# Another work order, a fourth load buffer and three conditioning pieces on TensorE in a hybrid decoder layer

## The chip, the cores and the metric

One core of one Trainium2 chip runs the whole layer. The metric is device time in microseconds (us), the lower the better. Five engines run their own instruction queues in order and wait for each other by semaphores: PE (TensorE, matmuls), DVE (VectorE), ACT (ScalarE), POOL (GpSimd) and SP (SyncE), which here issues nearly all DMA transfers.

## The reference

A decoder layer for 256 tokens of width 1024, in float32. A vector c gives six vectors (shift, scale and gate for two sublayers). The first sublayer is a token mixer with four gated DeltaNet heads and four HGRN2 heads, the second a mixture of 64 experts, 8 per token, with one shared expert. Cut to what matters:

```python
mod = c_act @ w_ada + b_ada                     # c_act = silu(c); w_ada is 1024 x 6144
sh1, sc1, g1, sh2, sc2, g2 = split(mod, 6)
h = rms_norm(x, norm1_w) * (1 + sc1) + sh1
x = x + g1 * token_mixer(h)                     # below
h = rms_norm(x, norm2_w) * (1 + sc2) + sh2
x = x + g2 * moe(h)                             # sigmoid router, top 8 of 64, plus a shared expert
return rms_norm(x, final_norm_w)

def token_mixer(h):
    proj = h @ w_in                             # 1024 -> q, k, v, gate A, beta, a, f, i, q B, gate B
    q, k, v = causal_short_conv(proj[:1536])    # 4 taps, silu
    oA = gated_delta_chunked(l2(q), l2(k), v, g, beta)       # chunks of 64, triangular solve
    oA = rms_norm(oA) * silu(gateA)
    oB = hgrn2_chunked(silu(qB), kB, iB, logf)               # kB, logf from sigmoid(f)
    oB = rms_norm(oB) * silu(gateB)
    return concat(oA, oB) @ w_out
```

## The kernel before

The kernel has two stages, the mixers and the experts.

**Mixers.** All work up to the residual behind the out-projection is cut into small pieces. Each piece is a step of a Python generator (up to its next `yield`), and the string `SEQ` names the generators in the order in which their steps are written: `W4` splits a block of w_in's rows, `Q4` multiplies it, `c1` is a step of a conditioning piece, `s_f0` a split of a weight tile, `inv` a step of the triangular inverse, `g0` and `g1` steps of the HGRN2 recurrence. Since each engine runs its queue in order, `SEQ` sets what stands before what on every engine. The table `ENG` says for some element-wise steps whether DVE or POOL does them, and `BANKS` which pair of PSUM banks a step uses.

Weights come in halves of 1 MB (128 partitions x 2048 floats), two halves to a tile `ld`, of which there are three buffers. They are queued on SP in the order in which `SEQ` first names them, and `take` issues them up to `NLD` = 6 halves ahead of the one that is needed. A tile takes the buffer of the tile three before it, so a load may stand on SP until that buffer has been read.

To keep float32 precision at the speed of the rounded type, a weight is split: ACT casts the high part (L451, L428) and DVE or POOL subtracts it for the low part (L452, L429). Three matmuls (high x high, high x low, low x high) then make each product: `first_columns` (L438, tiles `pqk`) for the first 1024 columns of w_in, 8 row blocks of 24 matmuls each, and `piece` (L477) for v, f, qb, i, gA and gB.

The conditioning has two halves. sh1 and sc1 are needed before the first projection: `ada` (L395) multiplies the blocks A0 to A3 of w_ada by c, 16 matmuls with 32 output columns each (32 passes on the array in the timeline's count), copies the sums (L398) and turns them to columns (L402); block Aq gives the columns of row blocks 2q and 2q + 1 of h. The other four vectors are made by eight pieces c0 to c7 (`cond`, tiles `ldc`): ACT scales the first slab, then seven steps on DVE add the others,

```python
S.activation(pa, t[:, :, 0, :], AF.Copy, scale=cact[:, 0:1])                      # L874
for j in range(1, 8):
    engine(f"c{n}", "V").scalar_tensor_tensor(pa, t[:, :, j, :], cact[:, j:j + 1], pa, ...)  # L877
TE.matmul(pc, lhsT=ones, rhs=pa, start=True, stop=True)                           # L880
V.tensor_tensor(dst, dst, two(pc), op=ALU.add)                                    # L882
```

`ba` (L496) makes beta and the decay, `ml` (L599) and `dec` (L616) the decay matrices, `LB` (L646) masked blocks for the inverse, `hT` (L413) the low part of h, `sgt` (L905) the gates' product, `out_part` (L1035) the out-projection, `xa` (L1063) a product of the second norm, whose result is `hpt` (L1070).

**Experts.** Behind the second norm the routing is computed (transposes L1159, logits L1227), while PE does the shared expert's gate and up (L1185); its weights take the tile `wbl0`, which reuses a load buffer (L1141, L1142). The weights of two experts are loaded ahead of the routing (`gu` and `wbl`, L995). Then 49 planned places are filled with the experts that are used, in the order of their load: gate, up and down matrices of 1 MB each stream through six pairs of buffers (`wbl`, `wbp`, `gu`) and five for the down matrices (`wbs`, `wbd`, `dn`), issued by L1370 to L1385, and the helper at L1399 does the matmuls. The last norm ends the kernel.

Of the kernel before, what the change touches and what calls it, by code (L numbers as in the profile page):

```python
# [40 lines left out]
NLD = 6  # L41
# [29 lines left out]
)  # L71

ENG = {
# [86 lines left out]
def tile_layer(ctx, tc, x, small, rows, w_ada, w_in, w_out, b_ada, gdn_norm_w, hg_norm_w, norm2_w, w_router, router_bias,  # L160
# [36 lines left out]
    x_sb = keep.tile([P, 2, D], F32, name="x_sb")  # L197


    loads, tiles, issued = [], {}, [0]  # L200

    def queue(key, half, src):
        loads.append((key, half, src))

    def issue(upto):
        while issued[0] < min(upto, len(loads)):
            key, half, src = loads[issued[0]]
            if half is None:
# [1497 lines left out]
```

## Time and profile before

| | us |
|---|---|
| median of 3 runs (lowest, highest) | 651.94 (649.45, 652.8) |
| the profiled execution, whole | 653.51 |
| its span in the trace | 651.6 |
| busy: PE, weight loads, DVE, ACT, POOL | 591.7, 367.4, 300.3, 209.8, 122.8 |

The shares of the whole span hide that the stages differ: DVE has 46% of the span, but most of that lies in the first third. The rows further below are therefore read stage by stage: the front (until the first projection is done, 61.6 us), the middle (the rest of the mixers, until the last out-projection matmul at 233.0), the tail (until the routing is known and the first planned expert load is issued, 256.4), and the experts. A row of a timeline that has x32 stands for 32 instructions, its first start and the time from there to the last end.

### The profile page before, as it was taken

The numbers are of one execution on the slowest core, as the hardware profiler recorded it, in microseconds if no ns is written. First come the engines' busy times: TensorE is split into PE (matmuls) and PEld (weight loads), VectorE is DVE, ScalarE is ACT, GpSimd is POOL, SyncE is SP. The second block draws the span as 40 slices with busy tenths as digits, with TensorE's granted clock in tenths as the row PEclk, the third lists the DMA queues.
The fourth block names the chain that finished last, engine by engine and source line by source line (L and its number), as shares of the span: only waits on it lengthen the run. The fifth ranks groups of instructions, "written<-read, shape, count | busy, mean of one in ns | idle before, by whom it ended". The sixth has DMA issues, their size and how long they took to land.

```text
span 651.6 us, 13055 instructions
## 1 busy us (share of the span) xinstructions
PE 591.7 (91%) x5317; PEld 367.4 (56%) x5318; DVE 300.3 (46%) x608; ACT 209.8 (32%) x409; POOL 122.8 (19%) x150
## 2 busy tenths in 40 slices
PE   3799887778898969999999999999999999999982
PEld 1499877777797957644445555444444444555321
DVE  4368999969899866112122221212221212221144
ACT  3356786535375451111112122121211111112112
POOL 7025255536474632000000000000000000000001
PEclk9889998969999989999999999999999999999997
DMA  8986563626638393999999999999999999999961
GB/s 344 422 336 245 194 259 130 208 82 233 257 132 351 135 351 137 421 391 412 420 420 419 420 420 420 420 418 417 420 420 418 421 419 420 419 418 420 418 228 69
DMA packets 32739, 216.78 MB, mean 333 GB/s; under 512 B 3792, under 2 KB 4128, under 8 KB 7456
## 3 DMA queue, kind: packets, MB, share of 16 engines
q1 hardware_dynamic: 32576, 215.83, 81.7%
q8 instruction: 44, 0.72, 0.5%
q14 instruction: 23, 0.19, 0.1%
q10 hardware_dynamic: 96, 0.04, 0.0%
HBM read 214.81 MB, written 1.05 MB: 331 GB/s over the span
## 4 chain that ended last, share of the span: by engine, by line
PE 62%; DVE 18%; DMA 13%; issue 3%; ACT 2%; SPq 1%; DVEq 0%; ACTq 0%
PE pgum L1399 21%; PE pym L1399 11%; PE pgm L1399 6%; PE acc L1399 6%; DVE pacc L877 4%; PE pqk L438 3%; DMA ldA<-in_w_ada_dram 3%; DMA wbl<-in_w_up_dram 3%; DMA wbp<-in_w_up_dram 3%; DMA wbd<-in_w_down_dram 3%; DVE cacc L542 2%; DVE wps L452 2%; PE i L477 2%; PE pgs L1185 2%; PE gA L477 2%
## 5 line engine op out<-in xcount | busy, mean ns | idle before, releaser
L1399 PE MATMUL pgum<-wbl,xgm 128*32 128x512 f32 (+1 forms) x768 | 155.3, 593 | 0.0
L1399 PE MATMUL pgum<-wbp,xgm 128*32 128x512 f32 (+1 forms) x448 | 98.7, 593 | 1.1 <-DMA wbp<-in_w_up_dram 1.1
L1399 PE MATMUL pym<-wbs,hTtm 128*32 128x512 f32 (+1 forms) x288 | 83.5, 596 | 0.5 <-ACT hTtm L1508 0.5
L1399 PEld LDWEIGHTS pgum<-wbl,xgm 128*32 128x32 f32 (+1 forms) x768 | 43.0, 113 | 67.3 <-issue 66.5
L1167 DVE TENSOR_TENSOR hhm<-sgm,pgum 128x256 f32<-128x256 f32 x24 | 14.9, 619 | 140.7 <-ACT sgm L1165 140.7
L1569 POOL TENSOR_TENSOR o<-x_sb,fbc 128x512 f32<-128x512 f32 x2 | 2.5, 1272 | 385.2 <-DVE x_sb L1551 385.2
L1535 DVE SCALAR_TENSOR_TENSOR ylm<-pym,gcm,yhm 128x512 fp32r<-128x512 f32 x46 | 34.6, 751 | 69.1 <-ACT yhm L1534 69.1
L1399 PE MATMUL pgum<-gu,xgm 128*32 128x512 f32 (+1 forms) x160 | 63.5, 593 | 0.0
L1399 PE MATMUL pym<-wbd,hTtm 128*32 128x512 f32 (+1 forms) x296 | 61.7, 595 | 0.5 <-ACT hTtm L1508 0.5
L1165 ACT ACTIVATE sgm<-pgum 128x256 f32<-128x256 f32 x24 | 9.2, 385 | 154.8 <-PE pgum L1399 154.8
L877 DVE SCALAR_TENSOR_TENSOR pacc<-ldc,cact,pacc 128x512 f32<-128x512 f32 x56 | 56.5, 1009 | 1.0
L1534 ACT ACTIVATE yhm<-pym,gcm 128x512 fp32r<-128x512 f32 x46 | 31.6, 688 | 76.1 <-PE pym L1399 76.1
L1399 PEld LDWEIGHTS pgum<-wbp,xgm 128*32 128x32 f32 (+1 forms) x448 | 26.4, 113 | 39.6 <-issue 39.6
L1399 PE MATMUL pym<-dn,hTtm 128*32 128x512 f32 (+1 forms) x104 | 43.5, 596 | 0.0
L1399 PE MATMUL pgm<-smm,h2hi 128*128 128x256 f32 x192 | 43.3, 305 | 0.0
L1399 PE MATMUL pgm<-smm,h2lo 128*128 128x256 f32 x192 | 38.2, 280 | 0.0
L1399 PE MATMUL acc<-yhm,stm 128*128 128x512 f32 x98 | 34.0, 427 | 0.0
L1399 PEld LDWEIGHTS pym<-wbs,hTtm 128*32 128x32 f32 (+1 forms) x288 | 20.2, 113 | 21.5 <-issue 19.5
L1399 PE MATMUL acc<-ylm,stm 128*128 128x512 f32 x94 | 29.9, 396 | 0.2 <-DVE ylm L1532 0.2
L1399 PEld LDWEIGHTS pgm<-smm,h2lo 128*128 128x128 f32 x192 | 29.5, 188 | 0.2 <-issue 0.2
L1399 PEld LDWEIGHTS pgm<-smm,h2hi 128*128 128x128 f32 x192 | 29.4, 189 | 0.3 <-issue 0.2
L1399 PEld LDWEIGHTS acc<-yhm,stm 128*128 128x128 f32 x98 | 16.5, 188 | 22.8 <-issue 18.8
(458 smaller groups left out, 1073.0 us busy)
## 6 DMA issues: line engine op xcount, KB each, us to landing
wbl<-in_w_gate_dram SPq DMA_DIRECT2D x25, 1024.0 KB, 17.4
wbl<-in_w_up_dram SPq DMA_DIRECT2D x25, 1024.0 KB, 19.4
wbs<-in_w_down_dram SPq DMA_DIRECT2D x19, 1024.0 KB, 15.4
wbd<-in_w_down_dram SPq DMA_DIRECT2D x19, 1024.0 KB, 19.2
wbp<-in_w_gate_dram SPq DMA_DIRECT2D x17, 1024.0 KB, 17.5
wbp<-in_w_up_dram SPq DMA_DIRECT2D x17, 1024.0 KB, 19.5
ldc<-in_w_ada_dram SPq DMA_DIRECT2D x16, 1024.0 KB, 7.9
dn<-in_w_down_dram SPq DMA_DIRECT2D x10, 1024.0 KB, 16.5
```

What stands on the lines that cost most here:

```text
L438: TE.matmul(pqk[m // 2][:, (m % 2) * T:(m % 2) * T + T], lhsT=ws[j][PAIRS[k][0]][:, m * P:m * P + P], rhs=hT[:, PAIRS[k][1], j, :], start= ...
L452: engine(f"s_{key}{q}", "GGVG"[q]).tensor_tensor(lo, t[:, 2 * q:2 * q + 2, :], hi.bitcast(F32), op=ALU.subtract)
L477: TE.matmul(pj[:, i * T:i * T + T], lhsT=lh, rhs=rh, start=(i == 0 and j == 0 and k == 0), stop=(i == 1 and j == 7 and k == 2), skip_group ...
L542: V.scalar_tensor_tensor(acc, xp[:, k:k + T], convcol[:, 12 * k + blk:12 * k + blk + 1], acc, op0=ALU.mult, op1=ALU.add)
L877: engine(f"c{n}", "V").scalar_tensor_tensor(pa, t[:, :, j, :], cact[:, j:j + 1], pa, op0=ALU.mult, op1=ALU.add)
L1165: S.activation(sg, pgate[:, 0:FE], AF.Silu)
L1167: V.tensor_tensor(hh.rearrange("p j q -> p q j"), sg.rearrange("p (q j) -> p q j", j=2), pgate[:, FE:2 * FE].rearrange("p (q j) -> p q j", ...
L1185: TE.matmul(pg2[:, i * FE:i * FE + FE], lhsT=hT_all[j // 4][:, j % 4, b * P:b * P + P], rhs=gu[:, i, j * FE:j * FE + FE], start=(j == 0 an ...
L1399: last_pe[0] = fn(*args, **kw).ins
L1534: S.activation(yh, pyd, AF.Copy, scale=gc)
L1535: V.scalar_tensor_tensor(yl, pyd, gc, yh.bitcast(F32), op0=ALU.mult, op1=ALU.subtract)
L1569: G.tensor_tensor(o[b, n], x1[:, b, sl], fbc[:, sl], op=ALU.mult)
```

## The change

The string `SEQ`, the tables `ENG` and `BANKS` are replaced as wholes, and with them the order of all the mixers' work. Of the split subtractions 11 instead of 19 are on DVE and 53 instead of 45 on POOL. On POOL instead of DVE are also one `xa` product, one `dec` product, two `LB` products and one `hT` subtraction; on DVE instead of POOL two of the `ml` products and one `sgt` product. `FIRST` orders the row blocks of the first projection: 6, 7, 4, 5, 0, 1, 2, 3. There are four buffers of load tiles, and `NLD` is 8; a load is written only where the last step that reads its buffer's previous tile stands ahead of it in `SEQ` (`lastread`). The conditioning pieces c0, c1 and c6 (`COND_PE`) are made by 16 matmuls, a copy by ACT, two matmuls that gather the sums, and the same addition as before. In the experts' stage one pair of buffers comes from the load pool instead of its own; there are six as before.

```diff
--- before.py
+++ after.py
-NLD = 6
+NLD, NLDBUF = 8, 4
...
-    "ba z0 par par par x A3 x xT0 xT0 A3 A3 xT1 xT1 A2 A2 A2 xT3 xT3 h7 xT2 h7 xT2 h5 h5 A0 A0 A0 h1 h1 h4 h4 z0 "
...
+    "par par x x xT0 xT3 xT1 xT3 A3 xT2 A3 A3 xT2 A2 h6 h6 h7 A2 W6 h7 A2 h4 xT1 Q6 W7 Q6 Q6 z0 A1 Q7 A1 xT0 Q7 A1 h5 Q7 W4 "
...
+COND_PE = (0, 1, 6)
+
+FIRST = (6, 7, 4, 5, 0, 1, 2, 3)
...
-    ld = ctx.enter_context(tc.tile_pool(name="load", bufs=3))
+    ld = ctx.enter_context(tc.tile_pool(name="load", bufs=NLDBUF))
...
-    loads, tiles, issued = [], {}, [0]
+    loads, tiles, issued, wanted = [], {}, [0], [0]
+    slots, lastread = [], {}
 
     def queue(key, half, src):
         loads.append((key, half, src))
 
-    def issue(upto):
+    def issue(upto, at=None):
+
         while issued[0] < min(upto, len(loads)):
             key, half, src = loads[issued[0]]
             if half is None:
                 row_loads(key)
             else:
                 if key not in tiles:
+                    if at is not None and len(slots) >= NLDBUF and lastread[slots[-NLDBUF]] > at:
+                        return
+                    slots.append(key)
                     tiles[key] = ld.tile([P, 2, 8, 256], F32, name=f"ld{key}", tag="ld")
                 SY.dma_start(out=tiles[key][:, half, :, :].rearrange("p j n -> p (j n)"), in_=src)
             issued[0] += 1
 
     def take(key, half, shape=None):
         n = next(n for n, l in enumerate(loads) if l[:2] == (key, half))
-        issue(n + NLD)
+        issue(n + 1)
+        wanted[0] = max(wanted[0], n + NLD)
         return half is not None and tiles[key][:, half, :, :]
+
+
+    count = {}
+    for place, op in enumerate(SEQ.split()):
+        seen = count.get(op, 0)
+        count[op] = seen + 1
+        if op[0] == "A" and op[1:].isdigit() and seen == 0:
+            lastread[op] = place
+        elif op[0] == "W" and seen == 0:
+            lastread[f"W{int(op[1:]) // 4}"] = place
+        elif op[:2] == "s_" and seen == 3:
+            lastread[op[2:-1]] = place
+        elif op[0] == "c" and op[1:].isdigit() and seen == (0 if int(op[1:]) in COND_PE else 7):
+            lastread[op] = place
+        elif op[0] == "y" and op[1] in "AB" and seen == 1:
+            lastread[f"wo{int(op[2]) // 2}"] = place
...
-    issue(NLD)
+    issue(NLD, 0)
+    wanted[0] = NLD
...
-    crep = tmp.tile([P, 8, 32], F32, name="crep", tag="a0")
+    crep = cp.tile([P, 8, 32], F32, name="crep")
...
-        if j in (3, 7):
-            hi, lo = (ep.tile([P, 1024], F32R, name=f"spw{j}{n}", tag=tag) for n, tag in enumerate(("attT", "LT")))
+        place = FIRST.index(j)
+        if place in (3, 7):
+            hi, lo = (ep.tile([P, 1024], F32R, name=f"spw{place}{n}", tag=tag) for n, tag in enumerate(("attT", "LT")))
         else:
-            if j == 2:
+            if place == 2:
                 w = mp.tile([P, 2, 1024], F32R, name="spw2", tag="kv8")
             else:
-                w = sps[(0, 1, 0, 0, 0, 1, 0)[j]].rearrange("p (a n) -> p a n", a=2)
+                w = sps[(0, 1, 0, 0, 0, 1, 0)[place]].rearrange("p (a n) -> p a n", a=2)
...
-                          start=(m % 2 == 0 and j == 0 and k == 0), stop=(m % 2 == 1 and j == 7 and k == 2), skip_group_check=True)
+                          start=(m % 2 == 0 and j == FIRST[0] and k == 0), stop=(m % 2 == 1 and j == FIRST[-1] and k == 2), skip_group_check=True)
...
+        if n in COND_PE:
+            pm = bank(f"cm{n}", "pm")
+            for j in range(4):
+                for g in range(4):
+                    k = 4 * (g % 2) + j
+                    TE.matmul(pm[32 * g:32 * g + 32, 0:256], lhsT=crep[:, k, :], rhs=t[:, g // 2, k, :], start=(j == 0), stop=(j == 3))
+            yield
+            pmc = tmp.tile([P, 256], F32, name=f"pmw{n}", tag="cacc")
+            (V.tensor_copy if ENG.get(f"cm{n}") == "V" else S.copy)(pmc, pm[:, 0:256])
+            yield
+            pc = bank(f"c{n}", "pm")
+            for i in range(2):
+                TE.matmul(pc[:, 256 * i:256 * i + 256], lhsT=pick[:, i:i + 1].to_broadcast([P, P]), rhs=pmc, start=True, stop=True)
+            yield
+            V.tensor_tensor(dst, dst, two(pc), op=ALU.add)
+            return
...
-                              start=(nm == "B" and n % 2 == 0 and j == 0 and k == 0), stop=(nm == "A" and n % 2 == 1 and j == 3 and k == 2),
-                              skip_group_check=True)
+                              start=(npy[n // 2, b] == 0), stop=(npy[n // 2, b] == 47), skip_group_check=True)
+                    npy[n // 2, b] += 1
...
-    for op in SEQ.split():
+    for place, op in enumerate(SEQ.split()):
         if op not in started:
             started[op] = WORK[op]()
         next(started[op], None)
+        issue(wanted[0], place)
...
-    lds = [ld.tile([P, 2, 2048], F32, name=f"wbl{k}", tag="ld") for k in range(3)]
-    wps2 = [wp2.tile([P, 2, 2048], F32, name=f"wbp{k}", tag="wp", bufs=2) for k in range(2)]
-    pairs = [lds[0], ahead[0][0], lds[1], wps2[0], wps2[1], lds[2]]
+    lds = [ld.tile([P, 2, 2048], F32, name=f"wbl{k}", tag="ld") for k in range(4)]
+    pairs = [lds[0], ahead[0][0], lds[1], lds[2], wp2.tile([P, 2, 2048], F32, name="wbp"), lds[3]]
...
-    sr = tmp.tile([P, 2, NE], F32, name="sr", tag="sr", bufs=1)
+    sr = tmp.tile([P, 2, NE], F32, name="sr", tag="m8", bufs=1)
```

SP's queue at the start of the program, weight loads of w_ada (A, c) and w_in (W, f); x2 means both halves, 1 MB each. Before:

```order
L213 DMA ldA3_100<-in_w_ada_dram 128x2048 x2
L213 DMA ldA2_103<-in_w_ada_dram 128x2048 x2
L213 DMA ldA0_106<-in_w_ada_dram 128x2048 x2
L213 DMA ldA1_228<-in_w_ada_dram 128x2048 x2
L213 DMA ldW0_271<-in_w_in_dram 128x2048 x2
L213 DMA ldc0_318<-in_w_ada_dram 128x2048 x2
L213 DMA ldW1_354<-in_w_in_dram 128x2048 x2
```

After:

```order
L220 DMA ldA3_100<-in_w_ada_dram 128x2048 x2
L220 DMA ldA2_103<-in_w_ada_dram 128x2048 x2
L220 DMA ldW1_106<-in_w_in_dram 128x2048
L220 DMA ldA1_108<-in_w_ada_dram 128x2048 x2
L220 DMA ldW1_106<-in_w_in_dram 128x2048
L220 DMA ldA0_253<-in_w_ada_dram 128x2048 x2
L220 DMA ldW0_286<-in_w_in_dram 128x2048 x2
L220 DMA ldc0_432<-in_w_ada_dram 128x2048 x2
```

W1, whose half with row blocks 6 and 7 now comes before A1, stood behind all four A tiles, W0 and c0; A0 now comes after A1 and all of W1.

POOL's queue where the f, qb and v projections begin (`wps` is the low part of a split weight, `ldf`, `ldqb`, `ldv` its source, T5, L5 and X32 tiles of the inverse). Before:

```order
L452 TENSOR_TENSOR wps0_81<-ldf_460,wps0_81 128x512
L452 TENSOR_TENSOR wps1_82<-ldqb_463,wps1_82 128x512
L632 MEMSET T5_207 128x1024
L632 MEMSET L5_208 128x512
L452 TENSOR_TENSOR wps0_81<-ldf_460,wps0_81 128x512
L452 TENSOR_TENSOR wps1_82<-ldf_460,wps1_82 128x512 x2
L452 TENSOR_TENSOR wps0_81<-ldqb_463,wps0_81 128x512
L452 TENSOR_TENSOR wps1_82<-ldqb_463,wps1_82 128x512 x2
L616 TENSOR_TENSOR dec_726<-dec_726,lex_123 128x4x128
L452 TENSOR_TENSOR wps0_81<-ldv_900,wps0_81 128x512
L646 TENSOR_TENSOR LB_205<-LT_203,bd32_146 128x128 x2
```

After:

```order
L478 TENSOR_TENSOR wps0_81<-ldf_436,wps0_81 128x512
L658 MEMSET T5_345 128x1024
L478 TENSOR_TENSOR wps0_81<-ldf_436,wps0_81 128x512
L478 TENSOR_TENSOR wps1_82<-ldqb_501,wps1_82 128x512 x2
L478 TENSOR_TENSOR wps0_81<-ldf_436,wps0_81 128x512 x2
L478 TENSOR_TENSOR wps1_82<-ldqb_501,wps1_82 128x512 x2
L642 TENSOR_TENSOR dec_728<-dec_728,lex_126 128x4x128
L478 TENSOR_TENSOR wps0_81<-ldf_436,wps0_81 128x512
L658 MEMSET L5_346 128x512
L478 TENSOR_TENSOR wps0_81<-ldf_436,wps0_81 128x512
L691 COPY X321_937<-ident32_148 128x256
L478 TENSOR_TENSOR wps0_81<-ldqb_501,wps0_81 128x512
```

Ahead of the first `LB` product, which waits for DVE, there were eight splits of f and qb; now there are thirteen, and with them a split of v, two `dec` products and the copy X32 among them.

PE's queue at the end of the mixers (`py` are the out-projection's sums, `ph` the second norm's transposes, `pgs` the shared expert's gate). Before:

```order
L1035 MATMUL py00_2548<-wps1_82,oTA_2727 128x256 x12
L1035 MATMUL py10_2583<-spoA20_2561,oTA_2727 128x256 x6
L1035 MATMUL py10_2583<-spoA21_2628,oTA_2727 128x256 x6
L1035 MATMUL py10_2583<-spoA30_2642,oTA_2727 128x256 x6
L1035 MATMUL py10_2583<-spoA31_2697,oTA_2727 128x256 x6
L1159 MATMUL ph00_2945<-ident_109,hpt_2873 128x128 x4
L1159 MATMUL ph01_2951<-ident_109,hpt_2873 128x128 x4
L1159 MATMUL ph10_2957<-ident_109,hpt_2873 128x128 x4
L1159 MATMUL ph11_2963<-ident_109,hpt_2873 128x128 x4
L1185 MATMUL pgs0_2941<-wbl0_2909,hpt_2873 128x256
```

After:

```order
L1078 MATMUL py00_2563<-wps1_82,oTA_2700 128x256 x12
L1078 MATMUL py10_2657<-spoA30_2713,oTA_2700 128x256 x6
L1078 MATMUL py10_2657<-spoA20_2583,oTA_2700 128x256 x6
L1078 MATMUL py10_2657<-spoA31_2763,oTA_2700 128x256 x6
L1078 MATMUL py10_2657<-spoA21_2697,oTA_2700 128x256 x6
L904 MATMUL cm6_2885<-ldc6_2248,crep_163 32x256 x16
L911 MATMUL c6_2904<-pmw6_2902,pick_173 128x256 x2
L1202 MATMUL ph00_2978<-ident_112,hpt_2863 128x128 x4
L1202 MATMUL ph01_2984<-ident_112,hpt_2863 128x128 x4
L1202 MATMUL ph10_2990<-ident_112,hpt_2863 128x128 x4
L1228 MATMUL pgs0_2974<-wbl0_2942,hpt_2863 128x256
L1202 MATMUL ph11_2996<-ident_112,hpt_2863 128x128 x4
```

The matmuls of c6 now stand between the last out-projection matmul and the transposes, and the first `pgs` matmul, which reads `wbl0`, ahead of the last transposes.

## Rows read from the trace of the kernel before

**Rows 1.** Windows by stage: busy us (x instructions) of each engine, granted clock, DMA share, GB/s.

```profile
32.80:61.60 28.80, 28.80 (x222) 27.55 (x223) 21.47 (x34) 15.87 (x23) 9.46 (x8) 0.93 0.71 274
...
233.00:256.40 23.40, 17.08 (x98) 13.22 (x98) 14.88 (x63) 9.23 (x16) 7.68 (x5) 0.93 0.61 248
256.40:624.20 367.80, 366.08 (x2743) 176.66 (x2742) 84.26 (x180) 69.89 (x133) 0.00 (x0) 1.00 1.01 416
624.20:651.60 27.40, 14.54 (x102) 5.08 (x102) 10.51 (x22) 6.89 (x15) 2.50 (x2) 0.87 0.28 103
```

**Rows 2.** Chain of waits, its end: start us, us, what.

```profile
604.14 19.93 DMA wbp<-in_w_up_dram
...
624.20 7.04 PE pgum L1399 x58
```

**Rows 3.** Timeline of PE, front: start, us, line, out<-in, count [idle before <-releaser].

```profile
17.10 1.93 PE L395 MATMUL A<-ldA,crep 128*32 128x256 f32 x32
...
27.78 3.62 PE L395 MATMUL A<-ldA,crep 128*32 128x256 f32 x28 [2.56 <-DMA ldA<-in_w_ada_dram]
...
32.81 7.72 PE L438 MATMUL pqk<-hT,wps 128*128 128x256 f32 x48
...
42.28 2.90 PE L496 MATMUL ba<-hT,wbs 128*8 128x256 f32 x24
```

**Rows 4.** Windows, the front's loads.

```profile
0.00:16.00 16.00, 5.89 (x37) 2.67 (x39) 6.71 (x22) 5.82 (x10) 12.47 (x55) 1.00 0.87 344
16.00:33.00 17.00, 12.62 (x127) 7.49 (x126) 6.40 (x19) 5.83 (x9) 1.62 (x2) 0.81 1.01 419
```

**Rows 5.** Timeline of ACT, front, the first projection's casts.

```profile
30.25 1.99 ACT L428 CAST wps<-ldW 128x1024 fp32r<-128x1024 f32 x2 [3.57 <-DMA ldW<-in_w_in_dram]
```

**Rows 6.** Windows, middle; the sum is of 61.6 to 233.

```profile
61.60:121.00 59.40, 51.72 (x575) 47.53 (x573) 56.45 (x107) 43.46 (x92) 28.11 (x26) 0.91 0.58 216
...
207.30:233.00 25.70, 25.04 (x202) 24.01 (x200) 23.21 (x42) 11.22 (x24) 13.23 (x11) 1.00 0.48 186
sum 171.40, PE 146.94 PEld 134.89 DVE 156.09 ACT 96.26 POOL 89.10; mean PE 36.73 PEld 33.72 DVE 39.02 ACT 24.07 POOL 22.27
```

**Rows 7.** Waits of PE, 61.6 to 233: us in total, times, longest.

```profile
PE u L757 <- DVE bv L769: 3.2, 1, 3.2
PE gB L477 <- DVE A L850: 3.1, 1, 3.1
```

**Rows 8.** Lines, 61.6 to 233: busy, mean ns of one, idle before.

```profile
L877 DVE SCALAR_TENSOR_TENSOR pacc<-ldc,cact,pacc 128x512 f32<-128x512 f32 x49 | 51.3, 1047 | 0.8
```

**Rows 9.** Window of line L452 alone: DVE busy, POOL busy, clock, DMA share, GB/s.

```profile
61.60:233.00 171.40, 18.07 (x19) 64.86 (x45) 0.94 0.54 203
```

**Rows 10.** Timeline of DVE and POOL, 78 to 91.

```profile
80.58 0.75 DVE L877 SCALAR_TENSOR_TENSOR pacc<-ldc,cact,pacc 128x512 f32<-128x512 f32 x1
...
86.44 3.00 POOL L452 TENSOR_TENSOR wps<-ldqb,wps 128x512 fp32r<-128x512 f32 x2 [0.72 <-PE ntk L569]
86.53 1.77 DVE L877 SCALAR_TENSOR_TENSOR pacc<-ldc,cact,pacc 128x512 f32<-128x512 f32 x1
```

**Rows 11.** Timeline of PE, tail.

```profile
238.41 3.58 PE L1159 MATMUL ph<-ident,hpt 128*128 128x128 f32 x16 [5.38 <-DVE hpt L1070]
241.83 0.60 PE L1185 MATMUL pgs<-wbl,hpt 128*128 128x256 f32 x2
```

**Rows 12.** Timeline of SP's queue, tail.

```profile
229.31 0.33 SPq L1141 DMA_DIRECT2D wbl<-in_ws_gate_dram  x1
```

**Rows 13.** DMA issues: count, KB each, us from issue to landing.

```profile
wbl<-in_ws_gate_dram SPq DMA_DIRECT2D x1, 1024.0 KB, 6.8
wbl<-in_ws_up_dram SPq DMA_DIRECT2D x1, 1024.0 KB, 9.0
```

**Rows 14.** Waits of POOL, whole span.

```profile
POOL wps L452 <- ACT wps L451: 57.1, 17, 7.1
...
POOL LB L646 <- DVE LT L642: 4.6, 2, 3.9
```

More of the change, by code (lines that the diff above doesn't have):

```diff
@@ L1012, in tile_layer @@
     py, xa = {}, {}
+    npy = {(m, b): 0 for m in range(2) for b in range(2)}
     def py_(m, b):
```

92 rows, old and new, of tables (BANKS, ENG, SEQ) are left out of this document.

## The prediction

> **What bounds the kernel now.** I read the windows by stage first, then the chain of waits, then the timeline of the front, and last the windows and waits of the middle. The windows show a kernel in two halves. From 256.4 to 624.2 us the DMA engines are full (share 1.01, 416 GB/s) [rows 1], and the chain there is one weight load after another until 624.20, where the last expert's matmuls start [rows 2]. That stage (367.8 us) and the 27.4 us behind it move the same bytes whatever comes before; nothing in the change alters them. It starts when the routing is known, at 256.4, because only then can the remaining expert loads be queued. So a microsecond that the mixers' stage gains at its end comes off the total, one for one, and the question is when the last out-projection matmul ends. Call that moment T; before, it is 233.0, the end of the window 207.3 to 233.
>
> **Front (to 61.6 us).** The first projection's 192 matmuls start at 32.81, behind the last conditioning block, whose 28 matmuls waited 2.56 us for their load [rows 3]. From there PE has no gap: 28.80 of 28.80 us busy [rows 1]. It is thus a load-bound front and then a PE-bound one, and the projection waits for 8 MB of conditioning weights (A3, A2, A0, A1) although its first row blocks need only some of them.
>
> After, the load order is x, A3, A2, half of W1, A1, the other half of W1, A0, W0, c0, and the blocks run 6, 7, 4, 5, 0 to 3. The first half of W1 ends at 1.05 + 2.1 + 2.1 + 1.05 = 6.3 MB. By 16.0 us 16.0 x 344 GB/s = 5.5 MB are in, and the rest at 419 GB/s takes 1.9 us [rows 4]: about 18. Two casts took 1.99 us [rows 5], then comes a subtraction: the projection starts at about 21, as an estimate. W0, the last it needs, ends at 13.6 MB, or 18 + 7.3/0.419 = 35.4, plus 2 for the casts: 37.4.
>
> PE's work from 21 on: the 192 matmuls are the 28.80 us of that window less 2.90 for ba [rows 3] and about 1.2 for two small ones, 24.7; ba 2.9; A1, A0 and the new c0 matmuls, 32 passes each at 1.93 us [rows 3], 5.8; the small matmuls between them 1.4. That is 34.8, so the front ends at 55.8 instead of 61.6: **-6**. W0 at 37.4 is met by half of that work, so it is just in time. Bounds: -1.5, if the loads share the engines, land later and the A blocks run as at 27.78 (28 passes in 3.62 us, rows 3) in a stretch with a mean granted clock of 0.81 [rows 4]; -8, if nothing of the sort occurs.
>
> **Middle (61.6 to 233.0, 171.4 us).** By the sum row DVE is busy 156.1 us (91%) and PE 146.9 (86%) [rows 6]. In the first window, 61.6 to 121, DVE is busy 56.45 of 59.4 us; PE's longest waits for another engine in the stage are for DVE (3.2 and 3.1) [rows 7]. DVE is the fuller engine.
>
> DVE loses: two of the pieces moved to TensorE lie here (c1 and c6; c0's lie in the front), 14 scalar-tensor-tensor at 1.047 [rows 8], 14.7 us; eight splits (19 to 11) at 18.07/19 = 0.951 [rows 9], 7.6; six small tensor operations that now run on POOL, 1.9. It gains three of the front's POOL operations (two ml, one gate product), about 2. Its work falls by 22 us to 134.
>
> Not all of that is saved, because DVE also gets slower. The same accumulation took 0.75 us with POOL idle, and 1.77 beside two POOL splits that run from 86.44 to 89.44 [rows 10]. POOL now gets eight splits more (45 to 53) and four small operations; each can stretch one DVE operation by 1.77 - 0.75 = 1.0 us, so 0 to +12; many fall beside DVE work that isn't stretched, so I take +6 and 140, or 82% of the old stage.
>
> PE gains the 16 matmuls of c1, 1.93 at the full clock; the two matmuls behind the copy take the place of the two that summed over partitions, and c6's lie after T. PE then has 148.9 and is the fuller engine. How much of the stage can the fuller one fill? The only measure is this stage: DVE filled 156.1/171.4 = 91%. So 148.9/0.91 = 163.6: **-7.8**. In other words PE's idle time falls from 24.5 us to 14.7; what goes is some ten of the microseconds that it waits for DVE. ACT loses three scalings and gains three copies, and at 96 of 171 us it hides either. What is late next is PE's own chains, the chunk inverse and the HGRN2 recurrence, and the casts. Bounds: +1.9 (no wait shrinks), and down to 150 us (-21, below).
>
> The fourth load buffer and the rule that a load is issued only once its slot's last reader is placed keep SP from standing behind a full slot. The trace of before does not show such a stall apart from the other waits. The nearest row is the 2.56 us by which a late load held PE in the front [rows 3]: a gain of 0 to 2.6 where one such wait goes, and as much lost where a load that is written later comes later. I take 0.
>
> **Tail (T to the routing).** c6's matmuls (1.93 to 3.62 by the two blocks above), its copy and pair of matmuls fall after T, in the 5.38 us for which PE waits for the second norm's hpt [rows 11]; they are hidden. But c6's weights hold a load buffer until those matmuls have read it, and the shared expert's gate and up weights take that buffer. Before, they were issued at 229.31, 3.7 us ahead of T, and landed 6.8 and 9.0 us later; they are first read at 241.83, T + 8.8 [rows 11 to 13]. After, they are issued at T + 2 to T + 3.6, and the gate half lands at T + 8.8 to T + 10.4, just late. On PE's queue the first matmul that reads it now stands ahead of the last transposes of the second norm, and behind these are the router's logits, so a late load delays the routing. One more xa product goes to POOL, where such an operation costs about 1.4 (64.86/45, rows 9) against 0.95. I take **+1.0**; bounds 0 and +4.
>
> **Sum**, against the profiled execution's 653.5 (span 651.6): -6 - 7.8 + 1 = -12.8, so 640.7. That execution lies 1.6 above the median of the runs, 651.94, so on the median: **639**.
>
> **Rivals.**
> B, PE's waits don't shrink. They are not all DVE's: the chains are serial, and an engine that becomes free finds the same chain. Against it: the two longest are DVE's, and the first stage has DVE at 95%. Then the middle costs +1.9, and the total is 653.5 - 6 + 1.9 + 1 = 650.4, or 649 on the median.
>
> C, slower: POOL becomes the engine that sets the pace of the split weights. In 61.6 to 121 POOL has 28.11 us [rows 6]; 14 instead of 8 of the f and qb splits, the eighth of v's, another dec and two LB products are 6 + 1 + 1 at 1.44 and two small ones, some 13 more, so 41 of 59. Its queue is in order, and a split stands behind products that wait: LB for LT 4.6 us [rows 14]. 41 and 4.6 leave it 13 us of that window for its waits for ACT's casts; where these and the like are more, POOL decides, and the f, qb and v projections end late: by 8 x (1.44 - 0.95) = 4 for the slower splits, plus a wait or two of that size, some 10 in all. 653.5 - 6 + 10 + 1 = 658.5, or 657. For it: the long queue. Against it: POOL was ahead of the projections for much of that stage, with 57.1 us in the kernel in which it waited for ACT's casts [rows 14]. The growth of a DVE operation beside a split, 1.0 us [rows 10], bears on it too. The Trainium skill, SBUF — State Buffer, section "Who interferes with whom", says that only the port pair shared by VectorE and GpSimd contends, and that it is an exclusive lock; the trace agrees for DVE by that 0.75 against 1.77. By the rule POOL would wait as well, up to 0.75 for each of the window's 26 operations and the ten more, and its 41 would be up to 68, more than the window, so that C would come. The row at 86.44 doesn't bear that half of it out: two splits beside DVE's work took 1.50 each, against a mean of 1.44.
>
> D, much faster: busy matmul time overstates PE, since its ends are modelled. By the weight loads PE has 134.89 us in the middle [rows 6], 79%; with c1 136.5. At 91% that is 150, T falls by 6 + 21, and the total by 26: 627.5, or 626 on the median. The Trainium skill, Trainium Kernel Development and Optimization, section "Performance Expectations", calls matmul busy time a bad metric and weight-load time a good one; no run here shows yet which of the two is the floor. Against D: in 207.3 to 233 PE is busy 25.04 of 25.70 by matmuls and 24.01 by weight loads [rows 6], and DVE still has 82% of the old stage.
>
> **How the numbers follow.** Forecast case 0.55 (own range 632 to 647), B 0.20, C 0.13, D 0.12. A difference of 0.5%, 3.3 us, is about what a measurement can tell from none here. B's 649 is on that bound: 0.08 of it counts as faster and 0.12 as the same; of C 0.02 is the same and 0.11 slower. Faster: 0.55 + 0.12 + 0.08 = 0.75; same 0.14; slower 0.11. The range 626 to 652 leaves out C and the lower half of D.
>
> **What would show it.** Front: the first projection's matmuls start near 21 and end near 56; if they start there and end at 60, the loads or the clock took it back. Middle: DVE's busy time near 140 and PE's idle time near 15 in a stage of some 164 us; an idle time that stays at 24 is B; POOL busy or waited for through the f, qb and v stage, with PE waiting for POOL's splits, is C. Tail: the shared gate's matmul starts within 1 us of the transposes; a gap there is the held buffer. The expert stage must again take 367.8 + 27.4 us at a full DMA share; if it doesn't, the first step is wrong. The prediction fails if the gain of the front is gone by T, or if the routing's start moves and the end does not.

## The result, and the profile after

The changed kernel took 641.25 us (median of four runs, 638.60 to 643.43) against 652.26 before: a ratio of 0.9853, 95% interval 0.982 to 0.9885. Run again beside the first experiments it took 639.49 (six runs, 636.68 to 640.02), ratio 0.9796 (0.976 to 0.9831). Forecast were 639 and "faster". The profiled execution took 643.43 with a span of 641.7; that of the second measurement, called the control below, 640.02 with 638.3.

Windows of the changed kernel by stage, with the same columns as [rows 1]: the first projection, the middle, the tail to the first planned expert load, the experts, the end.

```profile
21.30:57.40 36.10, 34.66 (x329) 30.01 (x329) 21.46 (x46) 17.09 (x26) 9.22 (x9) 1.00 1.01 413
57.40:223.00 165.60, 147.52 (x2034) 134.10 (x2036) 144.97 (x247) 97.04 (x208) 97.87 (x90) 0.97 0.51 197
223.00:247.00 24.00, 20.24 (x134) 15.08 (x135) 15.33 (x64) 9.02 (x16) 8.22 (x5) 0.93 0.60 240
247.00:614.75 367.75, 365.78 (x2742) 176.38 (x2742) 84.14 (x181) 69.86 (x133) 0.00 (x0) 1.00 1.01 416
614.75:641.70 26.95, 14.53 (x102) 5.08 (x102) 10.25 (x21) 6.88 (x15) 2.51 (x2) 0.87 0.26 95
```

Read against [rows 1, 6]: the experts take 367.75 us (367.80 before), and the last load's landing again releases the last expert (chain, as in [rows 2]):

```profile
594.61 20.00 DMA wbl<-in_w_up_dram
614.75 7.04 PE pgum L1442 x58
```

So the total moved by what lies ahead of 247.0, as the first step said. The front ends 57.5 instead of 61.6 (-4.1), the middle takes 165.5 instead of 171.4 (-5.9), the tail 24.0 instead of 23.35 (+0.65), the end 0.45 less: together -9.8, near the spans' difference of 9.9.

The same windows of the control show how much of this is chance:

```profile
20.70:59.20 38.50, 36.73 (x329) 31.03 (x329) 21.50 (x46) 17.22 (x26) 9.27 (x9) 0.96 1.01 410
59.20:220.80 161.60, 143.46 (x2033) 130.11 (x2035) 144.60 (x247) 96.88 (x208) 98.44 (x90) 1.00 0.51 198
220.80:243.90 23.10, 18.96 (x135) 13.85 (x135) 15.36 (x64) 8.95 (x17) 8.24 (x5) 1.00 0.62 249
```

The same program's middle took 161.6 us with a granted clock of 1.00 and 165.6 with 0.97; PE was busy 4 us less, DVE alike. A term read from one pair of profiles has 2 to 4 us of this in it. I therefore settle on medians of many runs and use the profiles for the place.

PE's front in the changed kernel (timeline as in [rows 3]): the projection starts at 21.30, and the only wait in it is for A0's second half.

```profile
21.30 3.09 PE L464 MATMUL pqk<-hT,wps 128*128 128x256 f32 x24
...
32.69 1.92 PE L420 MATMUL A<-ldA,crep 128*32 128x256 f32 x28 [1.44 <-DMA ldA<-in_w_ada_dram]
...
56.23 1.29 PE L464 MATMUL pqk<-hT,spw 128*128 128x256 f32 x8
```

PE's waits in the middle, 57.4 to 223 (us in total, times, longest), the three longest:

```profile
PE ia L703 <- DVE xp L562: 3.0, 1, 3.0
PE qk L677 <- DVE LT L669: 2.6, 1, 2.6
PE dec L636 <- ACT cacc L565: 2.5, 1, 2.5
```

All rows of that view together are 17.8 us (24.5 before), of which DVE ends 9.6 (16.6 before) and POOL 1.8 (none before). The two waits of [rows 7] are gone.

DVE's lines in the middle, of the changed kernel: the conditioning steps, and the convolution's steps, which the change leaves alone; then the latter's row of before.

```profile
L919 DVE SCALAR_TENSOR_TENSOR pacc<-ldc,cact,pacc 128x512 f32<-128x512 f32 x35 | 35.6, 1022 | 0.9 <-ACT pacc L916 0.8
L568 DVE SCALAR_TENSOR_TENSOR cacc<-xp,pcol,cacc 128x256 f32<-128x256 f32 x36 | 27.8, 786 | 4.1 <-ACT cacc L565 3.3
```

```profile
L542 DVE SCALAR_TENSOR_TENSOR cacc<-xp,pcol,cacc 128x256 f32<-128x256 f32 x36 | 23.4, 657 | 1.8 <-ACT xp L537 0.5 <-ACT cacc L539 0.2
```

The conditioning fell by 15.7 us, and the 36 convolution steps grew by 4.4. The split subtractions (view as in [rows 9]) went from 18.07 to 11.95 on DVE and from 64.86 to 72.14 on POOL:

```profile
57.40:223.00 165.60, 11.95 (x11) 72.14 (x51) 0.97 0.51 197
```

The tail of the changed kernel, first PE, then SP's queue (as in [rows 11, 12]):

```profile
222.92 1.93 PE L904 MATMUL cm<-ldc,crep 128*32 128x256 f32 x32
...
228.80 2.97 PE L1202 MATMUL ph<-ident,hpt 128*128 128x128 f32 x12 [1.57 <-DVE hpt L1113]
231.56 0.71 PE L1228 MATMUL pgs<-wbl,hpt 128*128 128x256 f32 x2
```

```profile
219.27 0.33 SPq L1184 DMA_DIRECT2D wbl<-in_ws_gate_dram  x1
...
224.53 0.34 SPq L1037 DMA_DIRECT2D wbl<-in_w_gate_dram  x1
```

The shared expert's gate is issued at 219.27, ahead of c6's matmuls at 222.92: it did not wait for them.

### The profile page after: what moved, and what is told of

Read it like the earlier page. It is cut to its first block, busy times and chain, and to the rows that moved or that the text cites. A ratio compares the mean times of both kernels' runs of the same rounds, so it can differ in the third digit from the quotient of the medians.

```text
span 641.7 us, 13236 instructions
## 1 busy us (share of the span) xinstructions
PE 592.9 (92%) x5419; PEld 367.0 (57%) x5420; DVE 284.3 (44%) x577; ACT 208.3 (32%) x410; POOL 130.3 (20%) x160
## 4 chain that ended last, share of the span: by engine, by line
PE 70%; DVE 14%; DMA 9%; ACT 3%; issue 2%; POOL 0%; SPq 0%; ACTq 0%; DVEq 0%
PE pgum L1442 24%; PE pym L1442 11%; PE pgm L1442 7%; PE acc L1442 6%; DMA wbl<-in_w_up_dram 6%; DVE cacc L568 3%; PE pqk L464 3%; DMA ldA<-in_w_ada_dram 2%; DVE pacc L919 2%; PE gA L503 2%; PE pgs L1228 2%; PE gB L503 2%; PE acc L1236 1%; PE phtm L1442 1%; PE i L503 1%
## 5 line engine op out<-in xcount | busy, mean ns | idle before, releaser
L1442 PE MATMUL pgum<-wbl,xgm 128*32 128x512 f32 (+1 forms) x944 | 170.3, 593 | 1.3 <-DMA wbl<-in_w_up_dram 1.3
L1442 PEld LDWEIGHTS pgum<-wbl,xgm 128*32 128x32 f32 (+1 forms) x944 | 48.5, 113 | 82.9 <-issue 82.9
L1442 PE MATMUL pgum<-wbp,xgm 128*32 128x512 f32 (+1 forms) x272 | 84.6, 593 | 0.0
L1577 ACT ACTIVATE yhm<-pym,gcm 128x512 fp32r<-128x512 f32 x46 | 31.6, 687 | 76.1 <-PE pym L1442 76.1
L919 DVE SCALAR_TENSOR_TENSOR pacc<-ldc,cact,pacc 128x512 f32<-128x512 f32 x35 | 35.6, 1022 | 0.9 <-ACT pacc L916 0.8
L1442 PEld LDWEIGHTS pgum<-wbp,xgm 128*32 128x32 f32 (+1 forms) x272 | 22.1, 113 | 24.2 <-issue 24.2
L568 DVE SCALAR_TENSOR_TENSOR cacc<-xp,pcol,cacc 128x256 f32<-128x256 f32 x36 | 27.8, 786 | 4.1 <-ACT cacc L565 3.3
## 6 DMA issues: line engine op xcount, KB each, us to landing
dn<-in_w_down_dram SPq DMA_DIRECT2D x10, 1024.0 KB, 16.6
```

The costliest lines, as they stand in the source:

```text
L568: V.scalar_tensor_tensor(acc, xp[:, k:k + T], convcol[:, 12 * k + blk:12 * k + blk + 1], acc, op0=ALU.mult, op1=ALU.add)
L1442: last_pe[0] = fn(*args, **kw).ins
L1577: S.activation(yh, pyd, AF.Copy, scale=gc)
```

## The experiments

Two questions were open: which part earned the 11 to 13 us, and whether the reasons given (PE held by DVE, the front one for one) are the right ones. The theory and its rivals stand with each run. Each was timed in 6 to 12 runs beside the kernel before, in three sets: the control, e1, e3 and e4 (median of before 652.47), e5, e6, e10 and e11 (650.22), and e7, e9, e13 and e14 (650.80). Across sets the ratios are to be compared and not the medians.

| kernel | median us | ratio to before (95%) |
|---|---|---|
| changed, first / control | 641.25 / 639.49 | 0.9853 (0.982-0.9885) / 0.9796 (0.976-0.9831) |
| e1: c0, c1 back on DVE | 647.72 | 0.9922 (0.9893-0.9951) |
| e3: old front | 647.44 | 0.9918 (0.9884-0.9951) |
| e4: split shares of before | 645.42 | 0.9895 (0.9862-0.9929) |
| e5: all shares and c0, c1 of before, new order | 649.44 | 0.9988 (0.9962-1.0015) |
| e6: before, with the new front | 651.33 | 1.0005 (0.9981-1.0029) |
| e14: before, with the fourth buffer | 649.54 | 0.9988 (0.9963-1.0013) |
| e7 / e9 / e13: c4 / c2 / both on TensorE too | 642.30 / 644.00 / 644.66 | 0.9862 / 0.9879 / 0.9889 |
| e10: changed, with dummy matmuls | 650.10 | 0.9979 (0.9957-1.0002) |
| e11: before, with dummy matmuls in the front | 651.21 | 0.9985 (0.9959-1.0011) |

**The control.** The kernel as changed.

> The changed kernel again, as the measure for the kernels that run beside it. Expected: 0.982 to 0.989 of the time before, some 641 us.

It came a little below the expected band, at 0.9796.

**e1: c0 and c1 on DVE again.**

```diff
-COND_PE = (0, 1, 6)
+COND_PE = (6,)
```

with c0's ten steps written together ahead of the decay products, and c1's within 50 steps of its first. Their place in the order changes with it, so the run undoes a little more than the engine.

> The changed kernel with c0 and c1 made by seven steps each on DVE again (their steps written close together, c0's ahead of the first decay products). Theory (the middle was paid by DVE): DVE gets 7 steps more in the front and 7 in the middle, and is again the fuller engine there, 145 + 7 = 152 of some 168 us, and the front's end waits for c0's: +4 to +9 us against the changed kernel. Rival (the new order did it, DVE's relief is spare): within 2 us.

It was 8.2 us slower than the control: the theory. Against the first profile most of what its own profile lost (4.4 us of span) lies early: v began at 98.1 instead of 94.5. Windows from the front's end to v's first matmul, of e1 and then of the changed kernel (PE, PEld, DVE, ACT, POOL, clock, DMA), and e1's middle:

```profile
58.30:98.00 39.70, 31.19 (x212) 27.16 (x210) 36.55 (x62) 28.81 (x60) 24.28 (x21) 0.96 0.47 184
```

```profile
57.50:94.50 37.00, 30.88 (x248) 27.46 (x246) 30.64 (x53) 29.30 (x63) 22.75 (x20) 1.00 0.52 207
```

```profile
58.30:227.20 168.90, 147.57 (x1998) 133.27 (x2000) 151.49 (x257) 97.44 (x208) 100.70 (x92) 0.96 0.50 191
```

DVE is 92% full there in e1 and 83% in the changed kernel. PE waited 3.64 us in one piece for a square that ACT makes of the convolution's result, which is DVE's work. Over the middle DVE is again the fuller engine, 151.49 of 168.90 us, as the theory had it (152 of 168).

**e3: the front of before in the changed kernel.**

```diff
-FIRST = (6, 7, 4, 5, 0, 1, 2, 3)
+FIRST = (0, 1, 2, 3, 4, 5, 6, 7)
```

and in SEQ, at the places of the front's steps, these steps in the order of before.

> The changed kernel with the front's steps in the order of before (loads A3, A2, A0, A1, W0, W1; row blocks 0 to 7), and all else as changed. Theory (the front's 4 us come off the end one for one): the first projection ends near 61.5 instead of 57.5 and the time is +3 to +5 us against the changed kernel. Rival (what the front gains is lost in the middle, where other waits decide): within 1.5 us.

It was 8.0 us slower than the control. Its first projection ended at 65.6, 6.4 us after the control's and 8.1 after the other profile's, later than before itself, also because c0's matmuls stand in it; its middle then took 163.6 us, between the two of the changed kernel (161.6 and 165.6):

```profile
32.60:65.60 33.00, 32.42 (x256) 30.18 (x257) 16.86 (x29) 14.48 (x21) 8.34 (x7) 0.88 0.83 323
65.60:229.20 163.60, 147.41 (x2033) 134.11 (x2035) 143.33 (x247) 96.97 (x208) 97.92 (x90) 0.97 0.51 197
```

By the medians, what the front loses in the new order comes through to the end: 8.0 us, for 6.4 or 8.1 at the front. (The profiles' spans differ by 8.1 and 4.7, so a single pair would not tell.) The direction is the theory's; the size, expected at 3 to 5, was not.

**e6: the new front in the kernel before.** The changed file with SEQ, ENG and BANKS of before, except for the front's steps and their banks, and

```diff
-COND_PE = (0, 1, 6)
+COND_PE = ()
```

> The kernel before with the front alone changed: loads A3, A2, W1, A1, A0, W0, row blocks from 6 on, the steps of the front in the changed order, four buffers and the rule that goes with them; all else (the order behind the front, DVE's and POOL's shares, all conditioning on DVE) as before. Theory (the front's gain comes off the end): -3 to -6 us against before. Rival (it is lost again, since the middle of before is paced by DVE and DVE's work has only moved): within 1.5 us.

No gain: the rival. The front did end at 58.6 instead of 61.6. But v began at 97.6 instead of 96.3 (windows from the front's end to there, of e6 and of before):

```profile
58.60:97.60 39.00, 32.83 (x232) 30.37 (x230) 34.46 (x60) 29.83 (x64) 18.31 (x14) 0.91 0.57 225
```

```profile
61.60:96.30 34.70, 30.29 (x231) 28.24 (x230) 32.79 (x61) 28.50 (x61) 14.88 (x12) 0.98 0.67 255
```

In the order of before DVE was busy 32.79 of 34.70 us in this stretch, and a first part of the gain is lost on it: three of its convolution steps took 3.25 us in e6 and 1.52 before, and by 67.9 us DVE was only 0.9 us ahead. The rest went another way. Behind a wait PE ran at a granted clock of 0.66, and DVE waited 3.04 us for a cast by ACT that followed PE's matmuls (0.42 before):

```profile
68.40:78.40 10.00, 8.06 (x41) 7.68 (x42) 6.53 (x13) 4.87 (x13) 1.69 (x2) 0.66 0.19 80
77.61 0.69 DVE L455 TENSOR_TENSOR wps<-ldf,wps 128x512 fp32r<-128x512 f32 x1 [3.04 <-ACT wps L454]
```

This profile fell on the slowest of the twelve runs, 656.64 us, so that stretch need not be typical. That the front's gain is gone in the order of before is shown by the times; that DVE's work alone takes it is not.

**e14: the fourth buffer alone.**

> The kernel before, in its own order and with its own front and shares of DVE and POOL, with the fourth buffer and with c0 and c1 made by TensorE: DVE's 14 steps for them are gone. Theory (DVE paces the middle of before, so its relief pays in any order): the middle gets 4 to 8 us shorter, time -3 to -8 us against before. Rival (relief pays only with the order that was made for it, as the new front by itself gave nothing): within 1.5 us.

The kernel that ran is not the one this speaks of: c0 and c1 stayed on DVE, as its 56 conditioning steps show (line view of the whole span):

```profile
L896 DVE SCALAR_TENSOR_TENSOR pacc<-ldc,cact,pacc 128x512 f32<-128x512 f32 x56 | 56.4, 1006 | 1.0
```

So it is the kernel before with the fourth buffer, the reach of 8 loads, the issue rule and the buffers that go with them: no change (0.9988, which is -2.4 to +0.8 us), within the term's bounds of 2.6 either way. What the relief of DVE does in the order of before was not tried.

**e4: the split shares of before.** ENG's entries for the split subtractions as before, 19 on DVE and 45 on POOL.

```diff
-"s_f00": "G", "s_qb00": "G", ... "s_yB33": "V", "s_yA00": "V", "s_yA31": "V"
+"s_f00": "V", "s_qb00": "V", ... "s_yB33": "G", "s_yA00": "G", "s_yA31": "G"
```

> The changed kernel with every split subtraction on the engine that it had before: 19 on DVE and 45 on POOL instead of 11 and 53. Theory (DVE's relief by the splits paid): DVE 145 + 7.6 less some 3 of contention = 149.6, as full as PE: +1 to +4 us. Rival (POOL's splits are slower and PE waits for them, so they cost): -1 to -3 us.

It was 5.9 us slower than the control, more than expected, and not for the reason given. DVE, with eight splits more, was busy 142.62 us in the middle, less than the 144.97 and 144.60 of the changed kernel. From the front's end to v's first matmul e4 took 37.5 us, the changed kernel 37.1 in both profiles; and gA's projection ended at 189.3, as in the control, though the front ended 1.7 us earlier (57.4; first profile: 57.4 and 191.4). What the profile shows of the loss comes behind gA (windows from there to the last out-projection matmul, e4 and control; the first profile has 31.6 us there):

```profile
189.30:224.40 35.10, 31.84 (x247) 30.22 (x249) 27.14 (x47) 15.74 (x32) 18.77 (x14) 0.95 0.49 193
```

```profile
189.30:220.80 31.50, 30.00 (x247) 28.42 (x249) 28.26 (x44) 15.73 (x32) 22.42 (x17) 1.00 0.55 214
```

There PE waits for a split that e4 gives back to POOL, and its next matmuls run at half the clock (10 in 2.50 us, 1.46 for ten in the control; granted clock 0.53 from 213.4 to 216.2; PE's timeline):

```profile
213.57 2.50 PE L1064 MATMUL py<-spoA,oTA 128*128 128x256 f32 x10 [2.74 <-POOL spoA L464]
```

So the seven f and qb splits that went to POOL earned at most 0.4 us up to v's start; which engine splits the out-projection's last weights earned 3.6. That belongs to the new order: before, PE's waits from 205 us to the end of the out-projection were 0.6 us in all.

**e5: the order without the relief.** e1 with the whole table ENG of before.

> The changed kernel with c0 and c1 on DVE and every element-wise step on the engine that it had before; the new order, the new front and the fourth buffer stay. Theory (relief of DVE and order belong together, each worth 6 to 8 us as the two kernels that undo one of them showed): 640 + 8 + 6 = 654, no faster than before. Rival (the two overlap: what one undoes, the other would have hidden): 645 to 649.

No faster than before, as the theory had it: 0.9988. Its 654 was 4.6 us high; 2.2 of these are the lower median of before in this set. By the ratios e5 lies 12.5 us above the control, where e1 and e4 add to 8.2 + 5.9 = 14.1. New order, new front and fourth buffer together give nothing with the old shares. It is not all DVE's doing: e4's wait for POOL's split at the out-projection is there again, 2.71 us, and PE was as busy as DVE in the middle (149.17 and 148.39 of 168.60 us).

**e7, e9, e13: further pieces on TensorE.** COND_PE = (0, 1, 4, 6), (0, 1, 2, 6) and (0, 1, 2, 4, 6), with banks to suit.

> The changed kernel with c4 on TensorE as well. c4's steps lie between 57 and 157 us, where TensorE has 83 to 84% and DVE 86 to 88%. Theory (there DVE still holds TensorE): DVE -7, PE +1.9, waits for DVE 9.6 to about 7: -1 to -4 us against the changed kernel. Rival (TensorE is now the fuller engine, so its added 1.9 us count): +1 to +3 us.

> The changed kernel with c2 on TensorE as well. c2's steps lie between 157 us and the end of the out-projection, where TensorE has 40.02 of 40.30 and 24.24 of 25.70 us. Theory (TensorE bounds that stretch): 0 to +2.5 us against the changed kernel. Rival (DVE's and POOL's late work still holds the out-projection): -1 to -4 us.

> The changed kernel with c2 and c4 on TensorE as well: if the two are independent, the sum of what each alone does, by the theories -1 to 0 us against the changed kernel.

None beats the changed kernel. e7's interval (0.9818 to 0.9906) holds the first measurement of the changed kernel and not the control's: c4 is worth nothing or costs, and a gain of 1 to 4 us does not show. e9 (0.9831 to 0.9927) and e13 (0.9848 to 0.993) lie above the control, by 5 to 6 us at the middle; from the first measurement, 2 us lower, they can't be told. In e9 PE is the fuller engine by far from 157 us on:

```profile
157.00:224.40 67.40, 65.54 (x635) 60.66 (x637) 48.23 (x80) 35.80 (x80) 37.27 (x36) 1.00 0.55 212
```

PE 65.5 of 67.4, DVE 48.2: here relief of DVE has little to buy, as the theory said. That the added matmuls are what costs is likely, and not shown by itself.

**e10: dummy matmuls in the changed kernel.**

```diff
+    def fill(dst, n):
+        for _ in range(n):
+            TE.matmul(dst, lhsT=ident, rhs=ident, start=True, stop=True)
...
         pa = bank(f"ia{i}", "pA")
+        if i == 1:
+            fill(pa[:, 0:P], 18)
```

> The changed kernel with dummy matmuls (128x128, read by nobody) on TensorE ahead of five steps for which it waits 1.4 to 3 us: 10 at A0, 16 at the first decay product, 18 at the inverse's first level, 10 at its last, 12 at the second norm's transposes. They lengthen no chain as long as they fit the wait. Theory (a wait of 2 to 3 us is followed by some us at half the clock, which costs as much again): the half-clock stretches behind these waits go, -1 to -4 us against the changed kernel. Rival (the clock doesn't matter here, or the dummies delay): -0.5 to +3 us.

A failed experiment: 12 us slower than the control by the ratios, because the dummies delayed. Two of their rows on PE's timeline:

```profile
58.15 3.73 PE L350 MATMUL dec<-ident 128*128 128x128 f32 x32
...
109.92 7.20 PE L350 MATMUL ia<-ident 128*128 128x128 f32 x36 [3.29 <-DVE xp L568]
```

The first decay product is not the one that waits, so 3.73 us were added there. At the inverse the dummies themselves waited 3.29 us. They read nothing but `ident`, which had long been there, so they waited for the PSUM bank that they and the step write to; the step's own wait thus ends with its bank too. It says nothing on the clock.

**e11: dummy matmuls in the front of before.** The same `fill`, 24 of them ahead of A1's matmuls.

> The kernel before with 24 dummy matmuls ahead of the A1 block, in the 2.56 us for which TensorE waits for its load; nothing else. Theory (the half clock from 26 to 36 us is due to that wait): the clock stays full there, the first projection ends some 3 us earlier, and the time is -2 to -4 us against before. Rival (the clock falls all the same, or the gain is lost in the middle): within 1 us.

The clock did stay full: windows of 26 to 36 us, of e11 and of before (PE, PEld, DVE, ACT, POOL, clock, DMA):

```profile
26.00:36.00 10.00, 9.37 (x93) 7.82 (x92) 3.58 (x9) 5.09 (x8) 1.62 (x2) 1.00 1.02 423
```

```profile
26.00:36.00 10.00, 7.69 (x47) 5.40 (x48) 3.78 (x9) 5.29 (x9) 1.62 (x2) 0.53 1.01 421
```

The 48 matmuls of [rows 3] at 32.81 took 6.63 us instead of 7.72. But they started 0.4 later, as the dummies outlasted the wait, the projection ended 0.7 earlier, and the time did not move (0.9985, 0.9959 to 1.0011): the rival. The half clock is not what the front of before loses its time by.

## Why the prediction was right

**The sum** (-12.8 by the profiled execution, 639 on the median) met -9.9 and -13.3 in the two profiles, 641.25 and 639.49 in the medians. **The first step**, all that counts lies ahead of the routing, held: the experts and the end took 394.7 and 394.4 us, against 395.2 before. The terms behind the sum fit less well than the sum.

**Front, -6.** Start 21 (measured 21.30) and 34.8 us of PE work (34.66) were right. Missed was A0: 2.1 MB ahead of W0's 35.4 it would have landed at 30.4; its last half came at 32.65 and cost the 1.44 us of the wait. Measured -4.1, and -2.4 in the control, where half the clock follows that wait (28 passes in 3.60 us, 1.92 in the first profile); both inside the bounds. "One for one" holds for the new order (e3) and not for that of before (e6). It was said for the stage's end and used for the front's: the step needed a condition that it did not name, a middle that can use the time. That the relief of DVE is this condition is likely, and not shown.

**Middle, -7.8.** PE's idle time fell from 24.5 to 17.8 and 17.6, not to 14.7; its busy time was 147.5 and 143.5 (148.9 forecast). Fill 89%, against the 91% used: measured -5.9 and -9.8. B is refuted: DVE's share of the waits fell by 7.0 of 16.6 (6.2 in the control). D is too: weight loads filled 134.10 of 165.60, 81%, against 79% before and D's 91%.

The sum held the clock fixed, and it was not: the middle's granted clock was 0.94 before [rows 9] and 0.97 and 1.00 after. With it PE's busy time came out 1.4 and 5.4 us under the forecast, while the waits fell by 6.7 and 6.9 instead of 9.8. That the two misses offset each other is luck. Over all runs of the control's set the mean granted clock of a run was 0.970 before and 0.988 after; how much of the 13 us this is, no run separates. It is not the gain by itself: e10 had 0.989, with its dummies, and no gain.

Mis-sized was **DVE's work after**, taken as 140 and measured 145. The conditioning fell by 15.7 (forecast 14.7) and the splits by 6.1 (7.6); but what the sum calls contention, taken as +6 of 0 to +12, came out as the remainder 145 - 134 = 11. The convolution gives 4.4 of it, 36 steps whose engine and shape nothing changed (657 to 786 ns), and there POOL is shown to be the cause: by the timelines of DVE and POOL laid side by side, 16 of them ran while POOL was idle and took 480 ns each, none over 487, and the 20 beside a POOL operation took 1031 on average. Before, it was 23 and 13. In e4, with the old shares, they are back near their old time:

```profile
L554 DVE SCALAR_TENSOR_TENSOR cacc<-xp,pcol,cacc 128x256 f32<-128x256 f32 x36 | 24.2, 687 | 1.2 <-ACT cacc L551 0.7
```

The other 6 or so are not traced to a cause. POOL's splits did not get slower: 72.14/51 = 1.41 us, against 1.44. And eight splits back on DVE made DVE no busier (e4). So the splits moved to POOL did not relieve DVE, and that step, "DVE loses 7.6", is right as a count and worth about nothing as a gain. The relief that paid is c0's and c1's (e1, 8.2 us). Beside these rows: the Trainium skill, SBUF — State Buffer, section "Who interferes with whom", says that a VectorE instruction with two inputs in SBUF contends with a GpSimd instruction that reads SBUF. The convolution's step has two, and the trace agrees (480 against 1031 ns).

**C, POOL paces the splits.** Not where it was put: PE waited 1.8 us for POOL in the whole middle. It is real at the out-projection, where e4 shows it (2.74 us in one wait).

**Tail, +1.0.** Measured +0.65 and -0.25. The mechanism was wrong: the shared expert's tile takes c2's buffer, not c6's. c6 was issued ahead of the two out-projection tiles, so of the last four tiles c2's is the oldest; c6 holds the buffer of the first expert loaded ahead, at 224.53 (T + 1.5; before 234.38, T + 1.4). The size was right by accident.

Still open: what c0 and c1 on TensorE give in the order of before, which was not run, and how the 11 to 13 us divide. Undone one at a time in the finished kernel, c0 and c1, the front and the split shares cost 8.2, 8.0 and 5.9 us, together more than the whole gain.

## What to carry to other kernels

Work brought forward can be worth nothing in the old order (e6) and 8 us in the finished kernel (e3): price a part in the order in which it will stand, and undo it from the finished kernel as well as adding it to the old one; the parts need not add up. Before crediting a move of element-wise work to POOL, subtract what it costs the DVE operations beside it; here DVE was no less busy with eight splits fewer. And read a profile's stages against a second profile of the same program before giving a cause for 3 us.

## What the runs showed of the hardware

The granted clock after the same wait differs from run to run. In both profiles of the changed kernel PE waited 3.03 us for the inverse's first level; from there on, 6.3 us of the first profile and of the control:

```profile
107.70:114.00 6.30, 6.20 (x154) 5.70 (x154) 5.97 (x11) 4.47 (x11) 3.99 (x3) 0.73 0.80 294
```

```profile
109.40:115.70 6.30, 5.00 (x154) 4.53 (x154) 5.97 (x11) 4.47 (x11) 4.01 (x3) 1.00 0.80 294
```

A granted clock of 0.73 as a mean (part of the stretch at 1.2 GHz, the rest at 2.4) in the one, 1.00 in the other, with the same 154 matmuls in the same 6.3 us: DVE was busy 5.97 us in both, and the difference did not show here. Over the whole middle the same program showed 0.97 and 1.00, and 4 us.
